# Gates and branches of the token mixers with the tokens' rows as the stationary operand and 512 weight columns moving

## The chip, the cores and the metric

The kernel runs on one core of a Trainium2 chip. The metric is the device time of one execution in microseconds (us). Three runs of the kernel before took 2425.22, 2427.73 and 2429.92 us; the median, 2427.73 us, is what the change is compared with.

## The reference

One decoder layer on 256 tokens of width 2048, all in float32. The part that the change touches is the merge of four token mixers ("branches", each 256 x 512) with sigmoid gates, and the projection behind it:

```python
h = adaLN(RMSNorm(x), c)                               # 256 x 2048
proj = h @ w_in                                        # nine slices of 512 columns feed four mixers
branches = (s5(...), hgrn2(...), stick_breaking(...), pool(...))     # each 256 x 512
terms = [sigmoid(h @ w_gate[n]) * (yb @ w_branch[n])   # w_gate[n] 2048 x 2048, w_branch[n] 512 x 2048
         for n, yb in enumerate(branches)]
merged = terms[0] + terms[1] + terms[2] + terms[3]     # 256 x 2048
x = x + gate_mix(c) * (merged @ w_out)                 # w_out 2048 x 2048
h = adaLN(RMSNorm(x), c); x = x + gate_ffn(c) * PEER(h)   # product-key experts; then a final RMSNorm
```

## The kernel before

**Layout and arithmetic.** Activations lie transposed: channels on the 128 partitions, tokens along the free axis, so `h` is 16 tiles of 128 channels x 256 tokens. A float32 product is made of three passes in the fp32r format. A weight tile of 128 x 1024 (512 KB) is loaded as `raw`, ScalarE copies it rounded to `hi` (line 186), VectorE subtracts to get `lo` (line 187); the helper is `split`. The activations are kept as `h_hi` and `h_lo` (the tile `hh`), the mixers' results as `yb[n]` (high and low, in slabs named `pj`). `gemm` then issues hi x high (line 192), hi x low (line 193) and lo x high (line 195). `raw` has 6 buffers, `hi` 4, `lo` 3; the weights stream through these, so ScalarE and VectorE can run ahead of TensorE by that many tiles and no further.

**Gate stage.** `gate_tile(n, m)` makes 128 gate channels for all 256 tokens: the weights are the stationary operand (128 x 128), 256 token columns move; 16 channel blocks times three passes are 48 matmuls into one PSUM tile (`gate_ps`, pool `psg`, two buffers), and ScalarE's sigmoid (line 826) evicts it. There are 4 x 16 = 64 gate tiles. `branch_tile(n, mq)` makes four such tiles `br_ps` of 12 matmuls each; VectorE multiplies each with the gate straight out of PSUM (lines 843 and 845) and adds into `merged` (line 846). For the last mixer (`n` = 0, the S5 one, worked last) the branch tiles lie in the pool `psv`, and `merged` is split into a high and a low part (`mg`, lines 850 and 851), which the product with `w_out` uses as its moving operand.

**Order.** The mixers are worked in the order 3, 2, 1, 0. A list goes over the 64 gate tiles; after each tile a fixed portion of the mixers' own work (`mixers`, `MIX_RATE`) and of a weight stream on VectorE (`ada`, line 243) is issued, and from the twelfth tile on, after every fourth, a branch of an earlier mixer tile group. Within an engine the framework's scheduler settles the order of what is ready; each engine then works its list strictly in order.

**After it.** `w_out` (16 output tiles `out_ps`, in `psg`), the second norm, the query projection, then the expert stages (`u_ps` and `v_ps`): those already have activations as the stationary operand and 512 weight columns moving, in the same fp32r format.

Of the kernel before, what the change touches and what calls it, by code (L numbers as in the profile page):

```python
# [19 lines left out]
D = 2048  # L20
T = 256
# [105 lines left out]
def emit(tc, ap, out):  # L127
# [8 lines left out]
    with ExitStack() as top:  # L136
# [139 lines left out]
        with ExitStack() as p1:  # L276
# [9 lines left out]
            def slab(dt=F32, shape=(128, 4, T)):  # L286
                return pj.tile(list(shape), dt, tag="pj", name="pj")
# [529 lines left out]
            merged = c1.tile([128, KT, T], F32, name="merged")  # L817
# [3 lines left out]
            def gate_tile(n, m):  # L821
                ps = psg.tile([128, T], F32, tag="g", name="gate_ps")
                gemm_tile(ps, ap["w_gate"][n, m],
                          lambda k: h_hi[:, k], lambda k: h_lo[:, k])
                sg = tp.tile([128, T], F32, tag="sig", name="sig", bufs=12)
                act(sg, ps, AF.Sigmoid)
                sig[n, m] = sg

            def branch_tile(n, mq):
                yh, yl = yb[n]  # L830
                for i in range(4):
                    m = 4 * mq + i
                    if i % 2 == 0:
                        hi, lo = split(ap["w_branch"][n, mq, i // 2])
                        hi = hi.rearrange("p (k m) -> p k m", k=4)
                        lo = lo.rearrange("p (k m) -> p k m", k=4)
                    msl = slice(i % 2 * 128, i % 2 * 128 + 128)
                    ps = (psg if n else psv).tile([128, T], F32, tag="v" if n == 0 else "g", name="br_ps")
                    gemm(ps, lambda k: hi[:, k, msl], lambda k: lo[:, k, msl],
                         lambda k: yh[:, k], lambda k: yl[:, k], range(4))  # L840
                    sg = sig.pop((n, m))
                    if n == 3:
                        tt(merged[:, m], sg, ps, op=ALU.mult)
                    else:
                        tt(sg, sg, ps, op=ALU.mult)
                        tt(merged[:, m], merged[:, m], sg, op=ALU.add)
                    if n == 0:
                        if i == 0:
                            mg[mq], mg[4 + mq] = slab(F32R), slab(F32R)
                        act(mg[mq][:, i], merged[:, m], AF.Copy)  # L850
                        tt(mg[4 + mq][:, i], merged[:, m], mg[mq][:, i].bitcast(F32),
                           op=ALU.subtract)
# [10 lines left out]
            order = [(n, m) for n in (3, 2, 1, 0) for m in range(KT)]  # L863
            for i in range(64 + 9):
                if i < 64:
                    gate_tile(*order[i])
                    mixers(MIX_RATE)
                    ada(ADA_RATE(i))
                if i >= 11 and (i - 11) % 4 == 0:
                    n, m = order[i - 11]  # L870
                    while n in left:
                        mixers.one()
                    branch_tile(n, m // 4)
# [16 lines left out]

            for m in range(KT):
                if m % 4 == 0:
# [3 lines left out]
                ps = psg.tile([128, T], F32, tag="g", name="out_ps")  # L896
                gemm_tile(ps, ap["w_out"][m],
                          lambda k: mg[k // 4][:, k % 4], lambda k: mg[4 + k // 4][:, k % 4])
# [455 lines left out]
def layout(i):  # L1354
# [11 lines left out]
    a["w_gate"] = f(i["w_gate"][0].reshape(4, KT, 128, KT, 128).transpose(0, 3, 2, 1, 4).reshape(4, KT, 128, 2048))  # L1366
    for n, k in (("w_out", "w_out"), ("w_query", "peer_w_query")):
        a[n] = f(i[k][0].reshape(KT, 128, KT, 128).transpose(2, 1, 0, 3).reshape(KT, 128, 2048))
    a["w_branch"] = f(i["w_branch"][0].reshape(4, 4, 128, 4, 2, 256).transpose(0, 3, 4, 2, 1, 5)
# [60 lines left out]
```

## Time and profile before

| what | value |
|---|---|
| median of three runs | 2427.73 us |
| the profiled execution | 2424.11 us, span 2422.3 us |
| TensorE busy | 2344.1 us, 97% of the span |
| VectorE busy | 2044.9 us, 84% |
| ScalarE busy | 1194.6 us, 49% |
| gate stage (first `gate_ps` to last `br_ps`) | 295.7 to 845.9 us |
| `w_out` | 844.5 to 946.7 us |
| DMA over the span | 678.43 MB, 280 GB/s |

[...] What a matmul costs in a stream is the distance from its start to the start of the next. The busy share of TensorE therefore says only that it is hardly ever left without work, and the time of an edit on it has to be read from start to start in a timeline. The other engines' busy times are plain.

### The profile page before, as it was taken

How to read it: one execution, taken by the hardware profiler on the slowest of the kernel's cores; microseconds unless marked ns; L12 is line 12 of the kernel's file. 1: busy time of each engine (PE TensorE's matmuls, PEld its weight loads, DVE VectorE, ACT ScalarE, POOL GpSimd, SP SyncE). 2: the span in 40 equal slices, each digit the busy share in tenths (PEclk: the TensorE clock that was granted, in tenths of full speed). 3: DMA queues.
4: the chain of work that ended last, by engine and by line, in shares of the span. 5: the costliest groups of instructions: out<-in, count | busy, mean ns of one | idle time of the engine just before them, and what ended most of it. 6: DMA issues, size and time to landing. Idle time of an engine off the chain costs nothing.

```text
span 2422.3 us, 39431 instructions
## 1 busy us (share of the span) xinstructions
PE 2344.1 (97%) x15282; PEld 2039.8 (84%) x15282; DVE 2044.9 (84%) x2999; ACT 1194.6 (49%) x1511; POOL 196.6 (8%) x132
## 2 busy tenths in 40 slices
PE   6999999999999999999899999999999999999997
PEld 4789999999999998988688888888888877878875
DVE  6666988779999887899977788888877899988986
ACT  4333466644444445555455544455555444455545
POOL 0000000000000000000122200011122101111110
PEclk9999999999999999999999999999999999999999
DMA  8977888866676686567799976789999767899973
GB/s 310 340 258 265 309 267 268 269 228 229 231 252 236 225 298 226 192 183 255 276 374 358 351 261 244 257 334 350 368 351 350 269 231 247 305 343 357 345 266 125
DMA packets 171724, 678.43 MB, mean 280 GB/s; under 512 B 18880, under 2 KB 23760, under 8 KB 154704
## 3 DMA queue, kind: packets, MB, share of 16 engines
q1 hardware_dynamic: 153104, 541.68, 64.1%
q0 software_dynamic: 18432, 134.23, 14.5%
q8 instruction: 120, 1.97, 0.3%
q14 instruction: 68, 0.56, 0.1%
HBM read 671.07 MB, written 4.20 MB: 279 GB/s over the span
## 4 chain that ended last, share of the span: by engine, by line
PE 82%; DVE 8%; DMA 5%; ACT 2%; issue 2%; SPq 0%; DVEq 0%; ACTq 0%
PE u_ps L1170 14%; PE u_ps L1175 9%; PE v_ps L1223 5%; PE v_ps L1224 5%; PE v_ps L1225 5%; PE v_ps L1228 5%; PE v_ps L1231 5%; DMA raw<-in_dram 4%; PE gate_ps L192 4%; PE gate_ps L193 3%; PE gate_ps L195 3%; PE w_ps L1141 3%; DVE lo L187 3%; PE psw_in L192 3%; PE psw_in L195 2%; PE psw_in L193 2%
## 5 line engine op out<-in xcount | busy, mean ns | idle before, releaser
L186 ACT ACTIVATE hi<-raw 128x1024 fp32r<-128x1024 f32 x808 | 854.9, 1060 | 1017.8 <-DMA raw<-in_dram 240.6
L187 DVE TENSOR_TENSOR lo<-raw,hi 128x1024 fp32r<-128x1024 f32 x808 | 978.3, 1219 | 199.0 <-ACT hi L186 170.2
L1097 POOL DMA_INDIRECT gat<-in_dram,sidx x128 | 196.4, 1534 | 2120.9 <-ACT ring L1196 1125.8
L1170 PE MATMUL u_ps<-hi,hd 128*128 128x512 f32 x1024 | 290.7, 402 | 0.6 <-ACT late L1184 0.6
L192 PE MATMUL gate_ps<-hh,hi 128*128 128x256 f32 x1024 | 256.0, 287 | 0.0
L193 PE MATMUL gate_ps<-hh,hi 128*128 128x256 f32 x1024 | 252.9, 284 | 0.0
L1170 PEld LDWEIGHTS u_ps<-hi,hd 128*128 128x128 f32 x1024 | 193.3, 195 | 39.9 <-ACT late L1184 6.7
L1223 PE MATMUL v_ps<-hi,ph 128*128 128x512 f32 x512 | 207.9, 408 | 6.1 <-DVE late L1240 3.4
L1225 PE MATMUL v_ps<-hi,ph 128*128 128x512 f32 x512 | 202.6, 396 | 0.0
L1224 PE MATMUL v_ps<-hi,ph 128*128 128x512 f32 x512 | 202.1, 395 | 0.0
L192 PEld LDWEIGHTS gate_ps<-hh,hi 128*128 128x128 f32 x1024 | 197.7, 193 | 3.1 <-issue 2.2
L243 DVE SCALAR_TENSOR_TENSOR pj<-raw,csil,pj 128x1024 f32<-128x1024 f32 x135 | 172.3, 1277 | 31.9 <-DMA raw<-in_dram 31.3
L193 PEld LDWEIGHTS gate_ps<-hh,hi 128*128 128x128 f32 x1024 | 197.8, 193 | 0.1
L1170 PE MATMUL u_ps<-lo,hd 128*128 128x512 f32 x512 | 163.6, 400 | 7.8 <-DVE lo L187 7.8
L1228 PE MATMUL v_ps<-lo,ph 128*128 128x512 f32 x512 | 162.9, 396 | 0.6 <-DVE lo L187 0.6
L1231 PE MATMUL v_ps<-lo,ph 128*128 128x512 f32 x512 | 162.8, 396 | 0.0
L1175 PE MATMUL u_ps<-hi,hd 128*128 128x512 f32 x512 | 161.5, 394 | 0.0
L1175 PE MATMUL u_ps<-lo,hd 128*128 128x512 f32 x512 | 159.5, 392 | 0.0
L1120 DVE SCALAR_TENSOR_TENSOR rows<-gat,dots,rows 128x2048 f32<-128x2048 f32 x63 | 147.7, 2345 | 0.0
L1110 DVE SCALAR_TENSOR_TENSOR gat<-gat,hrow 128x2048 f32<-128x2048 f32 x64 | 146.1, 2283 | 0.0
L195 PE MATMUL gate_ps<-hh,lo 128*128 128x256 f32 x1024 | 145.1, 284 | 0.0
L195 PEld LDWEIGHTS gate_ps<-hh,lo 128*128 128x128 f32 x1024 | 133.0, 193 | 0.3
(390 smaller groups left out, 4053.7 us busy)
## 6 DMA issues: line engine op xcount, KB each, us to landing
raw<-in_dram SPq DMA_DIRECT2D x1002, 512.0 KB
pj<-in_dram SPq DMA_DIRECT2D x10, 512.0 KB
x2d<-pj SPq DMA_DIRECT2D x4, 512.0 KB
ring<-in_dram SPq DMA_DIRECT2D x2, 1024.0 KB
gat<-in_dram,sidx POOLq DMA_INDIRECT x128, 8.3
xr<-x2d SPq DMA_DIRECT2D x8, 256.0 KB
ring<-g2d SPq DMA_DIRECT2D x1, 1024.0 KB
out_dram<-ring SPq DMA_DIRECT2D x4, 256.0 KB
```

Source lines behind the costliest of these rows:

```text
L186: act(hi, raw, AF.Copy)
L187: last["lo"] = tt(lo, raw, hi.bitcast(F32), op=ALU.subtract)
L192: mm(ps, hi(n), aH(k), start=start and n == 0, stop=False)
L193: mm(ps, hi(n), aL(k), start=False, stop=False)
L195: mm(ps, lo(n), aH(k), start=False, stop=stop and n == len(ks) - 1)
L1170: mm(ps0, hd[:, 2 * kk + i, 64:ND, r], w[:, i * 512:i * 512 + 512], start=kk == 0 and i == 0 and r == 0 and w is hi, stop=kk == 7 and i == ...
L1175: mm(ps1, hd[:, 2 * kk + i, 0:64].rearrange("p t r -> p (t r)"), w[:, i * 512:i * 512 + 512], start=kk == 0 and i == 0 and w is hi, stop=k ...
L1223: mm(vps[dq], phl[:, i, 0:128, 1], hi[:, dsl], start=first, stop=False)
L1224: mm(vps[dq], phl[:, i, 0:128, 0], hi[:, dsl], start=False, stop=False)
L1225: mm(vps[2 + dq], phl[:, i, 128:192].rearrange("p t r -> p (t r)"), hi[:, dsl], start=first, stop=False)
L1228: mm(vps[2 + dq], phl[:, i, 128:192].rearrange("p t r -> p (t r)"), lo[:, dsl], start=False, stop=last)
L1231: mm(vps[dq], phl[:, i, 0:128, 0], lo[:, dsl], start=False, stop=last)
```

## The change

The gates and the branches are turned round. A unit is 512 gate channels of one mixer, and it holds both halves of the tokens at once: two PSUM tiles of 128 tokens x 512 channels, which are all of `psg`. The stationary operand is 128 channels x 128 tokens of `h_hi` or `h_lo`, the moving one 512 columns of `hi` or `lo`. A unit takes 8 weight tiles and 96 matmuls; there are 16 units in place of 64 gate tiles. In the last of its 8 weight tiles the first token half is finished before the second. A branch unit takes 2 weight tiles and 24 matmuls, and its two PSUM tiles come from `psg` too (from `psv` for the last mixer). Sigmoids, products and sums are 128 x 512. `merged` then has tokens on the partitions, so 64 TensorE transposes of 128 x 128 turn it back (`turned`), and the split into `mg` reads their PSUM tiles. The transposes of the last quarter stand behind the first halves of two `w_out` tiles. The mixers' portions are issued after every second weight tile, which is the same pace as before. The weights lie in DRAM in the new order; bytes and number of loads are the same.

```diff
-            merged = c1.tile([128, KT, T], F32, name="merged")
+            merged = c1.tile([128, 2, D], F32, name="merged")
             mg = [None] * 8
             sig = {}
 
-            def gate_tile(n, m):
-                ps = psg.tile([128, T], F32, tag="g", name="gate_ps")
-                gemm_tile(ps, ap["w_gate"][n, m],
-                          lambda k: h_hi[:, k], lambda k: h_lo[:, k])
-                sg = tp.tile([128, T], F32, tag="sig", name="sig", bufs=12)
-                act(sg, ps, AF.Sigmoid)
-                sig[n, m] = sg
-
-            def branch_tile(n, mq):
+            def rows_gemm(ps, t, hi, lo, aH, aL, ks, start, stop, parts=(0, 1)):
+
+                tsl = slice(t * 128, t * 128 + 128)
+                for i, k in enumerate(ks):
+                    w = hi[:, i * 512:i * 512 + 512]
+                    if 0 in parts:
+                        mm(ps, aH(k)[:, tsl], w, start=start and i == 0, stop=False)
+                        mm(ps, aL(k)[:, tsl], w, start=False, stop=False)
+                if 1 in parts:
+                    for i, k in enumerate(ks):
+                        mm(ps, aH(k)[:, tsl], lo[:, i * 512:i * 512 + 512], start=False,
+                           stop=stop and i == 1)
+
+            def gate_unit(n, m4, side):
+                ps = [psg.tile([128, 512], F32, tag="g", name="gate_ps") for _ in range(2)]
+                aH, aL = lambda k: h_hi[:, k], lambda k: h_lo[:, k]
+                for u in range(8):
+                    hi, lo = split(ap["w_gate"][n, m4, u])
+                    ks = range(2 * u, 2 * u + 2)
+                    for p in ((0, 1),) if u == 7 else ((0,), (1,)):
+                        for t in range(2):
+                            rows_gemm(ps[t], t, hi, lo, aH, aL, ks, u == 0, u == 7, p)
+                    if u % 2:
+                        side()
+                for t in range(2):
+                    sig[n, m4, t] = tp.tile([128, 512], F32, tag="sig", name="sig", bufs=6)
+                    act(sig[n, m4, t], ps[t], AF.Sigmoid)
+
+            def turned(m4):
+
+                mg[m4], mg[4 + m4] = slab(F32R), slab(F32R)
+                for j in range(2):
+                    ps = psv.tile([128, 2, T], F32, tag="v", name="mg_ps")
+                    for i in range(2):
+                        d0 = m4 * 512 + j * 256 + i * 128
+                        for t in range(2):
+                            nc.tensor.transpose(ps[:, i, t * 128:t * 128 + 128],
+                                                merged[:, t, d0:d0 + 128], ident)
+                    sl = slice(2 * j, 2 * j + 2)
+                    act(mg[m4][:, sl], ps, AF.Copy)
+                    tt(mg[4 + m4][:, sl], ps, mg[m4][:, sl].bitcast(F32), op=ALU.subtract)
+
+            def branch_unit(n, m4):
                 yh, yl = yb[n]
-                for i in range(4):
-                    m = 4 * mq + i
-                    if i % 2 == 0:
-                        hi, lo = split(ap["w_branch"][n, mq, i // 2])
-                        hi = hi.rearrange("p (k m) -> p k m", k=4)
-                        lo = lo.rearrange("p (k m) -> p k m", k=4)
-                    msl = slice(i % 2 * 128, i % 2 * 128 + 128)
-                    ps = (psg if n else psv).tile([128, T], F32, tag="v" if n == 0 else "g", name="br_ps")
-                    gemm(ps, lambda k: hi[:, k, msl], lambda k: lo[:, k, msl],
-                         lambda k: yh[:, k], lambda k: yl[:, k], range(4))
-                    sg = sig.pop((n, m))
+                parts = [split(ap["w_branch"][n, m4, u]) for u in range(2)]
+                pool, tag = (psg, "g") if n else (psv, "v")
+                ps = [pool.tile([128, 512], F32, tag=tag, name="br_ps") for _ in range(2)]
+                for t in range(2):
+                    for u in range(2):
+                        rows_gemm(ps[t], t, *parts[u], lambda k: yh[:, k], lambda k: yl[:, k],
+                                  range(2 * u, 2 * u + 2), u == 0, u == 1)
+                    sg = sig.pop((n, m4, t))
+                    dst = merged[:, t, m4 * 512:m4 * 512 + 512]
                     if n == 3:
-                        tt(merged[:, m], sg, ps, op=ALU.mult)
+                        tt(dst, sg, ps[t], op=ALU.mult)
                     else:
-                        tt(sg, sg, ps, op=ALU.mult)
-                        tt(merged[:, m], merged[:, m], sg, op=ALU.add)
-                    if n == 0:
-                        if i == 0:
-                            mg[mq], mg[4 + mq] = slab(F32R), slab(F32R)
-                        act(mg[mq][:, i], merged[:, m], AF.Copy)
-                        tt(mg[4 + mq][:, i], merged[:, m], mg[mq][:, i].bitcast(F32),
-                           op=ALU.subtract)
+                        tt(sg, sg, ps[t], op=ALU.mult)
+                        tt(dst, dst, sg, op=ALU.add)
...
-            order = [(n, m) for n in (3, 2, 1, 0) for m in range(KT)]
-            for i in range(64 + 9):
-                if i < 64:
-                    gate_tile(*order[i])
-                    mixers(MIX_RATE)
-                    ada(ADA_RATE(i))
-                if i >= 11 and (i - 11) % 4 == 0:
-                    n, m = order[i - 11]
+            order = [(n, m4) for n in (3, 2, 1, 0) for m4 in range(4)]
+            beat = iter(range(64))
+
+            def step():
+                mixers(MIX_RATE)
+                ada(ADA_RATE(next(beat)))
+
+            for j in range(16 + 2):
+                if j < 16:
+                    gate_unit(*order[j], step)
+                if j >= 2:
+                    n, m4 = order[j - 2]
+                    if n == 0 and m4 > 0:
+                        turned(m4 - 1)
                     while n in left:
                         mixers.one()
-                    branch_tile(n, m // 4)
+                    branch_unit(n, m4)
...
+            ops = {}
             for m in range(KT):
                 if m % 4 == 0:
                     xq = slab()
                     load(out=xq, in_=ap["xT"][:, m:m + 4, :])
                     x2.append(xq)
-                ps = psg.tile([128, T], F32, tag="g", name="out_ps")
-                gemm_tile(ps, ap["w_out"][m],
-                          lambda k: mg[k // 4][:, k % 4], lambda k: mg[4 + k // 4][:, k % 4])
+                for i, halves in (((0, (0,)), (1, (0,)), (0, (1,))) if m == 0 else
+                                  ((1, (1,)),) if m == 1 else ((m, (0, 1)),)):
+                    if halves[0] == 0:
+                        ops[i] = psg.tile([128, T], F32, tag="g", name="out_ps")
+                    elif m == 0:
+                        turned(3)
+                    gemm_tile(ops[i], ap["w_out"][i],
+                              lambda k: mg[k // 4][:, k % 4], lambda k: mg[4 + k // 4][:, k % 4],
+                              halves)
+                ps = ops.pop(m)
...
-    a["w_gate"] = f(i["w_gate"][0].reshape(4, KT, 128, KT, 128).transpose(0, 3, 2, 1, 4).reshape(4, KT, 128, 2048))
+    a["w_gate"] = f(i["w_gate"][0].reshape(4, 8, 2, 128, 4, 512).transpose(0, 4, 1, 3, 2, 5)
+                    .reshape(4, 4, 8, 128, 1024))
-    a["w_branch"] = f(i["w_branch"][0].reshape(4, 4, 128, 4, 2, 256).transpose(0, 3, 4, 2, 1, 5)
+    a["w_branch"] = f(i["w_branch"][0].reshape(4, 2, 2, 128, 4, 512).transpose(0, 4, 1, 3, 2, 5)
```

On TensorE, here a branch of the second mixer and the gate tile or unit behind it. Before, each PSUM tile has its own name in the list, and the gate's one tile follows:

```order
L195 MATMUL br_ps_5816<-pj_3298,lo_5798 128x256 x4
L192 MATMUL gate_ps_5831<-hh_89,hi_5834 128x256
L193 MATMUL gate_ps_5831<-hh_89,hi_5834 128x256
...
L195 MATMUL gate_ps_5831<-hh_89,lo_5835 128x256 x8
```

Now (the first tile of each pair is the first token half, the second the second):

```order
L831 MATMUL br_ps_4945<-lo_4942,pj_3219 128x512 x2
...
L831 MATMUL br_ps_4946<-lo_4942,pj_3219 128x512 x2
L827 MATMUL gate_ps_4975<-hi_4979,hh_89 128x512
L828 MATMUL gate_ps_4975<-hi_4979,hh_89 128x512
...
L831 MATMUL gate_ps_4975<-lo_4980,hh_89 128x512 x2
L827 MATMUL gate_ps_4976<-hi_4979,hh_89 128x512
```

Where two PSUM tiles took turns, both now go to the gate unit at once: six matmuls into `gate_ps_4975` stand between the branch's last matmul and the first into `gate_ps_4976`, the buffer that VectorE has to have emptied of `br_ps_4946`.

On VectorE, the emptying of the same branch and what stands between. Before:

```order
L845 TENSOR_TENSOR sig_4840<-sig_4840,br_ps_5801 128x256
L643 SCALAR_TENSOR_TENSOR pj_5751<-hg_o_5577,col_105,pj_5751 128x256
L846 TENSOR_TENSOR merged_3059<-merged_3059,sig_4840 128x256
L845 TENSOR_TENSOR sig_4926<-sig_4926,br_ps_5816 128x256
L645 TENSOR_TENSOR pj_5751<-pj_5751,pj_151 128x256
L846 TENSOR_TENSOR merged_3059<-merged_3059,sig_4926 128x256
L187 TENSOR_TENSOR lo_6000<-raw_5997,hi_5999 128x1024
```

Now:

```order
L877 TENSOR_TENSOR sig_4404<-sig_4404,br_ps_4945 128x512
L647 TENSOR_TENSOR pj_4863<-pj_4921,pj_4862 128x512
L878 TENSOR_TENSOR merged_3059<-merged_3059,sig_4404 128x512
L187 TENSOR_TENSOR lo_4998<-raw_4995,hi_4997 128x1024
L877 TENSOR_TENSOR sig_4406<-sig_4406,br_ps_4946 128x512
L187 TENSOR_TENSOR lo_5118<-raw_5115,hi_5117 128x1024
L878 TENSOR_TENSOR merged_3059<-merged_3059,sig_4406 128x512
```

Two evictions of 512 columns stand where four of 256 stood, with a weight tile's `lo` between them.

On ScalarE, a gate's sigmoid and the weight tiles of later work that are rounded ahead of it. Before, behind the gate tile's own last weight tile `hi_5864`:

```order
L186 ACTIVATE hi_5999<-raw_5997 128x1024
L186 ACTIVATE hi_6029<-raw_6027 128x1024
L646 ACTIVATE pj_5665<-pj_5751 128x512
L186 ACTIVATE hi_6121<-raw_6119 128x1024
L186 ACTIVATE hi_6151<-raw_6149 128x1024
L826 ACTIVATE sig_5892<-gate_ps_5831 128x256
```

Now, behind the unit's own last weight tile `hi_5280`:

```order
L186 ACTIVATE hi_5342<-raw_5340 128x1024
L186 ACTIVATE hi_5348<-raw_5346 128x1024
L186 ACTIVATE hi_5386<-raw_5384 128x1024
L847 ACTIVATE sig_5336<-gate_ps_4975 128x512
L757 ACTIVATE pj_5297<-pj_5180 128x4x32
```

The sigmoid has moved from behind four later weight tiles to behind three. Between the last matmul of the first token half and the branch that follows, in the list of TensorE, stand five matmuls at least and mostly six to ten.

## Rows read from the trace of the kernel before

**Rows 1.** The page: TensorE's busy line, and the chain that ended last by engine.

```profile
PE 2344.1 (97%) x15282; PEld 2039.8 (84%) x15282; DVE 2044.9 (84%) x2999; ACT 1194.6 (49%) x1511; POOL 196.6 (8%) x132
PE 82%; DVE 8%; DMA 5%; ACT 2%; issue 2%; SPq 0%; DVEq 0%; ACTq 0%
```

**Rows 2.** Busy time in two stretches of the gate stage; columns in the first line.

```profile
core 0: us, PE busy (x) PEld busy (x) DVE busy (x) ACT busy (x) POOL busy (x), PEclk, DMA share, GB/s
296.00:540.00 244.00, 235.79 (x2305) 232.06 (x2304) 198.51 (x262) 152.19 (x185) 0.00 (x0) 1.00 0.78 257
540.00:790.00 250.00, 248.55 (x1969) 234.19 (x1968) 238.55 (x402) 111.49 (x169) 0.00 (x0) 0.99 0.70 238
```

**Rows 3.** Timeline of TensorE, half a gate tile: start, duration, line, tiles, count.

```profile
708.88 0.28 PE L192 MATMUL gate_ps<-hh,hi 128*128 128x256 f32 x1
...
710.80 1.12 PE L195 MATMUL gate_ps<-hh,lo 128*128 128x256 f32 x8
711.76 0.28 PE L192 MATMUL gate_ps<-hh,hi 128*128 128x256 f32 x1
```

**Rows 4.** Timeline of TensorE in the first expert stage, one weight tile.

```profile
1303.81 1.09 PE L1170 MATMUL u_ps<-hi,hd 128*128 128x512 f32 x4
...
1306.12 1.09 PE L1170 MATMUL u_ps<-hi,hd 128*128 128x512 f32 x4
```

**Rows 5.** Timeline of TensorE in the second expert stage, one weight tile.

```profile
2187.38 0.40 PE L1223 MATMUL v_ps<-hi,ph 128*128 128x512 f32 x1
...
2189.72 0.40 PE L1223 MATMUL v_ps<-hi,ph 128*128 128x512 f32 x1
```

**Rows 6.** Timeline of TensorE, four float32 transposes between the expert stages.

```profile
1586.30 0.60 PE L1191 MATMUL t_ps<-cst,late 128*128 128x128 f32 x4
1586.65 0.49 PE L1223 MATMUL v_ps<-hi,ph 128*128 128x512 f32 x1
1586.98 0.39 PE L1224 MATMUL v_ps<-hi,ph 128*128 128x512 f32 x1
```

**Rows 7.** Groups of instructions from 296 to 846: busy us, mean ns, idle before.

```profile
L192 PE MATMUL br_ps<-pj,hi 128*128 128x256 f32 x256 | 66.1, 292 | 7.6 <-DVE merged L843 4.9 <-ACT sig L826 2.3 <-ACT s5sg L811 0.4
L826 ACT ACTIVATE sig<-gate_ps 128x256 f32<-128x256 f32 x64 | 24.1, 377 | 29.0 <-PE gate_ps L195 28.7
L826 ACT ACT_TABLE_LOAD x18 | 23.1, 1283 | 0.3
L845 DVE TENSOR_TENSOR sig<-sig,br_ps 128x256 f32<-128x256 f32 x46 | 18.7, 413 | 3.8 <-PE br_ps L195 3.7
L846 DVE TENSOR_TENSOR merged<-merged,sig 128x256 f32<-128x256 f32 x46 | 18.5, 415 | 0.0
L781 DVE TENSOR_TENSOR s5a<-s5bu,pj 128x512 f32<-128x512 f32 x16 | 10.9, 683 | 2.0 <-PE s5bu L778 1.9
L851 DVE TENSOR_TENSOR pj<-merged,pj 128x256 fp32r<-128x256 f32 x13 | 5.3, 416 | 0.5 <-ACT pj L850 0.5
L639 ACT ACTIVATE pj<-hg_s 128x512 f32<-128x512 f32 x2 | 1.2, 595 | 1.3 <-PE hg_s L637 1.3
```

**Rows 8.** Groups of the whole program: the same transposes' mean duration.

```profile
L1191 PE MATMUL t_ps<-cst,late 128*128 128x128 f32 x128 | 19.3, 272 | 0.0
```

**Rows 9.** Timeline: a branch tile's last matmuls, and VectorE's eviction of it.

```profile
653.71 0.64 PE L195 MATMUL br_ps<-pj,lo 128*128 128x256 f32 x4
...
655.82 0.72 DVE L845 TENSOR_TENSOR sig<-sig,br_ps 128x256 f32<-128x256 f32 x2
```

**Rows 10.** Timeline: a gate tile's last matmuls, its sigmoid, the branch behind it.

```profile
684.42 1.12 PE L195 MATMUL gate_ps<-hh,lo 128*128 128x256 f32 x8
...
688.39 0.38 ACT L826 ACTIVATE sig<-gate_ps 128x256 f32<-128x256 f32 x1
...
688.83 0.38 PE L192 MATMUL br_ps<-pj,hi 128*128 128x256 f32 x1 [0.80 <-ACT sig L826]
```

## The prediction

> **What bounds the kernel now.** I began with the page: TensorE is busy 97% of the span, and the chain that ended last runs over it for 82% [rows 1]. A busy share that high leaves two questions, what a matmul costs from start to start and which other engine is close behind. The busy times of two stretches of the gate stage answer the second [rows 2]: from 296 to 540 us VectorE is busy 198.5 of 244 us and TensorE 235.8, so TensorE alone sets the pace; from 540 to 790 us, where the S5 mixer's work runs beside the gates, VectorE is busy 238.6 of 250 us, 95%, and TensorE 248.6. [...] The timeline gives the first answer: half a gate tile is 24 matmuls of 256 columns, and the next half starts 2.88 us after it [rows 3], 0.1200 us each. The idle time before the branches' matmuls is 7.6 us in all, put down to evictions of the PSUM tiles [rows 7]; the gates show none.
>
> **The matmuls.** Removed: 64 gate tiles of 48 and 64 branch tiles of 12, together 3840 of 256 columns; 3840 x 0.1200 = 460.8 us. Added: 16 units of 96 and 16 of 24, together 1920 of 512 columns. The kernel already has that form, activations stationary and 512 weight columns moving, each block of columns used by two matmuls in a row. In the first expert stage ten of them take 2.31 us, 0.2310 each [rows 4]; in the second 2.34 us, 0.2340 each [rows 5]. The product is 443.5 or 449.3 us. Nothing in the two stages says which the gates resemble more, so I take the middle, 0.2325 us: 446.4 us. That is **-14.4 us**, with ends -17.3 and -11.5. Pairs of 256 cost 0.240 and one of 512 costs 0.2325; half as many instructions buys only 3%. All of it lies on the engine that sets the end.
>
> **The transposes.** Added: 64 on TensorE, float32, 128 x 128. The nearest row is one of the same form: four transposes and one 512-column matmul behind them take from 1586.30 to 1586.98 us, 0.68 us [rows 6]. Less 0.234 for the matmul that is 0.446 us for four, 0.1115 each, and 64 make **+7.1 us**. The lower end is the four alone, 0.35 us, so 5.6 us in all. The upper end is no overlap at all: a mean duration of 272 ns [rows 8], 17.4 us. I take 7.1, since the starts show that they overlap.
>
> **The evictions.** On VectorE 64 products and 48 sums of 256 columns at 413 and 415 ns become 32 and 24 of 512 columns at 683 ns, the duration of a product out of PSUM of that size [rows 7]: 46.4 us become 38.2. The low parts of `merged` are 16 at 416 ns and become 8 at 683, 6.7 to 5.5. VectorE loses 9.4 us of work. On ScalarE 64 sigmoids at 377 ns become 32 at 595 (a copy out of PSUM of that size) [rows 7], 24.1 to 19.0, beside 18 table loads of 1.283 us which can only become fewer. I count all this as nothing, because TensorE's work covers it; if VectorE should be the one that binds from 540 us on, its own relief there is 0.6 us a unit (four products and four sums of 256 columns against two and two of 512), which is the first rival below.
>
> **The waits at the hand-over of PSUM.** A unit now holds both buffers of `psg`. Behind a branch the next unit's second half needs the buffer that VectorE empties last. Six matmuls stand between, 1.40 us. The result is there about 0.17 us after the last matmul's turn (a duration of 0.40 against a distance of 0.234 [rows 5]), and the product takes 0.683: VectorE may come 0.55 us late before TensorE stops. If it stops, the whole list behind it waits, and with it ScalarE and VectorE, once the four `hi` and three `lo` are full. There are 12 such places. The trace shows VectorE prompt at some and late at others: a branch tile that ended at 654.35 us was taken up at 655.82, 1.47 us late [rows 9]. The price at one place is between 0 and 0.92 us; I take 0.3, nearer to the prompt end, because VectorE has as a rule already waited for the first half of the same branch. Together 3.6 us, between 0 and 11.0.
>
> Before a branch, and between the first units, it is ScalarE that must have emptied the first half. With six matmuls between, 0.17 for the result and 0.595 for the sigmoid, it may come 0.63 us late. There are 14 such places. The trace has a gate tile that ended at 685.54 us and whose sigmoid began at 688.39, 2.85 us late, with 0.80 us of wait for the branch [rows 10]; behind the new order that would be 2.22 us. The sigmoid has moved forward by one weight tile in ScalarE's list, so I take 0.2 us a place, 2.8 us; the ends are 0 and, with half the places as late as that one, 15.5 us. In return the 7.6 us of old waits go. **-1.2 us** in all, between -7.6 and +18.9.
>
> **The rest.** Loads keep their number and size. The last quarter's transposes stand behind 31 matmuls of `w_out`, 3.7 us by 0.1200 each, in which the last product and sum, 0.17 + 0.683 + 0.683 = 1.5 us, fit with a weight tile's work between: nothing, and up to 2 us if VectorE comes late.
>
> **Sum.** -14.4 + 7.1 - 1.2 = -8.5 us. The profiled execution took 2424.11 us (its span 2422.3, with 1.8 around it) and would take 2415.6. It lies 3.6 us below the median of the runs, 2427.73; carried over to the median, the forecast is **2419 us**, 0.35% faster. A measurement of this kernel can tell about 0.2%, 4.9 us, from no change: faster is below 2422.9, slower above 2432.6.
>
> **Rivals.** *VectorE binds beside the S5 mixer.* At 95% busy for 250 of the stage's 550 us [rows 2], it could hold that stretch to its old length. Then the share 250/550 of 14.4 us, 6.5 us, is lost, and the sum is -2.0: 2426 us, no change. For it speaks the 95%; against it that TensorE is at 99% in the same stretch and that VectorE is relieved too.
>
> *The hand-over waits decide.* One mechanism: two halves that share two buffers stop TensorE at each unit's edge until VectorE or ScalarE has come round. With VectorE as late as in [rows 9] at all 12 places and ScalarE as late as in [rows 10] at seven of 14, the waits are 11.0 + 15.5 = 26.5 us and the sum is -14.4 + 7.1 + 26.5 - 7.6 = +11.6: 2439 us, slower. It makes the kernel slower than can be called no change from 19.8 us of waits on, 0.76 us at each of 26 places. For it speaks that lateness of 1 us and more is there in the trace; against it that the order now puts six matmuls and more into each gap.
>
> *The transposes do not overlap.* At 272 ns each [rows 8] they cost 17.4 us in place of 7.1, and the sum is +1.8: 2430 us. Against it speaks the distance of starts in [rows 6].
>
> [...]
>
> **Chances.** The forecast has 0.47, with its own range from 2410 to 2424; VectorE binding 0.27; the hand-over waits 0.18; the transposes 0.08. Of the forecast 0.43 lies below 2422.9 and 0.04 above; of VectorE's case 0.02 is faster, 0.23 the same, 0.02 slower; the waits are slower; of the transposes 0.05 is the same, 0.03 slower. So faster 0.45, same 0.32, slower 0.23. The best ends of all terms give -17.3 + 5.6 - 7.6 = -19.3, 2408 us; the worst -11.5 + 17.4 + 18.9 + 2 = +26.8, 2455 us. The range from 2407 to 2441 leaves out the worst part of the two slow cases.
>
> **What would show it.** Starts of `gate_ps` matmuls 0.231 to 0.234 us apart, against 0.120 for half the columns; more than 0.236 makes the first step wrong, and at 0.240 it is worth nothing. Groups of eight `mg_ps` transposes near 0.9 us. Idle time in front of `gate_ps` and `br_ps` matmuls near 6 us and put down to VectorE's products or ScalarE's sigmoids; above 20 us the second rival has won. If the starts are as forecast, the waits small and the stage from the first gate to the last branch still about 550 us long with VectorE at 97% or more from 540 us on, VectorE binds.

## The result, and the profile after

Six runs of the changed kernel have a median of 2411.23 us (2405.55 to 2415.05); six of the kernel before, on the same chip, 2427.85 us. The ratio is 0.9933, 95% interval 0.992 to 0.9945: 16.6 us faster. A second set on another chip gave 2412.31 us, ratio 0.9925 (0.9907 to 0.9944). The profiled run took 2414.72 us (span 2412.9), the profile of the second set has a span of 2409.1.

TensorE's line of the page, in place of the one in [rows 1], and the two stretches of [rows 2] again:

```profile
PE 2332.8 (97%) x13394; PEld 1942.4 (81%) x13394; DVE 2039.8 (85%) x2935; ACT 1173.5 (49%) x1458; POOL 199.4 (8%) x132
```

```profile
296.00:540.00 244.00, 232.57 (x1461) 190.24 (x1460) 198.52 (x251) 133.05 (x156) 0.00 (x0) 0.97 0.76 258
540.00:790.00 250.00, 245.85 (x1143) 189.24 (x1142) 242.39 (x383) 114.36 (x158) 0.00 (x0) 0.99 0.71 242
```

TensorE has 1888 records fewer and is still busy 97%. Yet it works less in both stretches than before (232.57 against 235.79, 245.85 against 248.55): it waits more. In the first one the granted clock has gone from 1.00 to 0.97. The groups from 295 to 838 us, which answer to [rows 7]:

```profile
L827 PE MATMUL gate_ps<-hi,hh 128*128 128x512 f32 x512 | 206.1, 403 | 10.3 <-DVE merged L875 6.4 <-ACT sig L847 3.9
L827 PE MATMUL br_ps<-hi,pj 128*128 128x512 f32 x128 | 52.7, 414 | 6.0 <-ACT sig L847 4.9 <-ACT pj L813 1.1
L847 ACT ACTIVATE sig<-gate_ps 128x512 f32<-128x512 f32 x32 | 18.4, 593 | 3.8 <-PE gate_ps L831 3.7
L877 DVE TENSOR_TENSOR sig<-sig,br_ps 128x512 f32<-128x512 f32 x23 | 15.6, 680 | 3.3 <-PE br_ps L831 3.0
L847 ACT ACT_TABLE_LOAD x11 | 14.1, 1283 | 0.2
```

Sigmoids and products cost what the rows of before had said (593 and 680 ns). The idle time before gates and branches has gone from 7.6 us to 16.3, and the gates, which had none, have most of it. Over the whole gate stage TensorE waited 11.7 us before, 16.7 now, and 15.9 in the second set.

The timeline of TensorE around one of the three long waits (start, duration, line, tiles, count, idle time before and what ended it):

```profile
612.36 0.39 PE L827 MATMUL gate_ps<-hi,hh 128*128 128x512 f32 x1
612.59 0.39 PE L828 MATMUL gate_ps<-hi,hh 128*128 128x512 f32 x1
612.81 0.39 PE L827 MATMUL gate_ps<-hi,hh 128*128 128x512 f32 x1
613.04 0.39 PE L828 MATMUL gate_ps<-hi,hh 128*128 128x512 f32 x1
613.27 0.61 PE L831 MATMUL gate_ps<-lo,hh 128*128 128x512 f32 x2
617.68 0.79 PE L827 MATMUL br_ps<-hi,pj 128*128 128x512 f32 x1 [3.80 <-ACT sig L847]
618.27 0.63 PE L828 MATMUL br_ps<-hi,pj 128*128 128x512 f32 x1
618.70 0.63 PE L827 MATMUL br_ps<-hi,pj 128*128 128x512 f32 x1
619.12 0.63 PE L828 MATMUL br_ps<-hi,pj 128*128 128x512 f32 x1
```

From 612.36 to 613.27 us four matmuls start 0.2275 us apart, though each lasts 0.39; the median over all 1920 is 0.227, less than either price of [rows 4, 5]. Then the branch waits 3.80 us for a sigmoid. Behind the wait the starts are 0.43 us apart, nearly twice as far, and the stretches of the profile say why (here the first wait, at 324 us; the column behind the busy times is the granted clock):

```profile
323.20:330.03 6.83, 6.00 (x14) 4.74 (x15) 5.15 (x7) 5.71 (x7) 0.00 (x0) 0.50 0.85 315
330.03:333.00 2.97, 2.97 (x14) 2.44 (x14) 0.41 (x2) 0.85 (x1) 0.00 (x0) 1.00 0.48 177
```

For 6.83 us the clock was granted at 0.50, then at 1.00. Such a stretch stands behind each of the three waits. Its first 0.8 to 0.9 us still lie in the wait, and of the other 6 us about half is lost, 3.0 us (by the starts, 0.43 us apart in place of 0.227, it is 2.8). The gate stage has three of them now, 20.5 us in all (10.2 in the second set). The gate stage of before has one, 6.8 us from 636.6 us on, with no wait in the 8 us ahead of it: TensorE was busy all of that time, from 635.09 us on with 16 matmuls of a single column, 13 of which began ahead of the stretch. So a wait is not the only thing in front of such a stretch.

The three waits have three causes. At 617.68 ScalarE comes late, behind eight scaled copies of the S5 mixer (line 765) and a table load:

```profile
612.86 2.86 ACT L765 ACTIVATE s5e<-pj,s5pw 128x128 f32<-128x128 f32 x8
615.74 1.28 ACT L847 ACT_TABLE_LOAD   x1
617.03 1.08 ACT L847 ACTIVATE sig<-gate_ps 128x512 f32<-128x512 f32 x2
```

At 324.03 (3.71 us) it is ScalarE too, with two table loads around the stick-breaking mixer's own function ahead of the sigmoid. At 487.93 it is VectorE, whose product (line 875) stands in its list behind a weight stream (line 243) that waits 3.33 us for its load:

```profile
484.86 1.28 DVE L243 SCALAR_TENSOR_TENSOR pj<-raw,csil,pj 128x1024 f32<-128x1024 f32 x1 [3.33 <-DMA raw<-in_dram]
486.06 1.22 DVE L187 TENSOR_TENSOR lo<-raw,hi 128x1024 fp32r<-128x1024 f32 x1
487.20 0.68 DVE L875 TENSOR_TENSOR merged<-sig,br_ps 128x512 f32<-128x512 f32 x1
```

The transposes, eight of a quarter and the branch behind them:

```profile
816.70 1.03 PE L857 MATMUL mg_ps<-cst,merged 128*128 128x128 f32 x8
817.49 0.48 PE L827 MATMUL br_ps<-hi,pj 128*128 128x512 f32 x1
817.81 0.40 PE L828 MATMUL br_ps<-hi,pj 128*128 128x512 f32 x1
```

From 816.70 to 817.81 us are 1.11 us; less 0.227 for the branch's matmul, 0.110 us for each transpose. There are four such groups, 32 transposes. The 64 of the section on the change and of the prediction was a miscount: four quarters, two PSUM tiles, two channel blocks and two token halves are 32.

**The sum.** At the median distance, 1920 x 0.227 = 435.8 us stand against 460.8: -25.0. But in either kernel some hundred of these matmuls, most of them next to a matmul of other work or to a wait, take 0.06 us or more longer than that to the next start. Added up from start to start, without idle time and without what the slow clock cost (estimated as half of each stretch, less its part in a wait), the gates and branches fall from 470.2 us to 449.4 (449.7 in the second set): -20.8 and -20.5. The whole gate stage, from the timelines, in us:

| first `gate_ps` to last `br_ps` | before | changed | second set |
|---|---|---|---|
| length | 550.2 | 543.0 | 538.8 |
| gates and branches, start to start | 470.2 | 449.4 | 449.7 |
| idle time of TensorE | 11.7 | 16.7 | 15.9 |
| lost to the slow clock | 3.4 | 8.9 | 5.0 |
| transposes (24 of the 32) | 0 | 2.2 | 2.2 |
| first matmuls of `w_out` | 0.3 | 2.3 | 2.3 |
| the mixers' own matmuls | 64.7 | 63.5 | 63.6 |

Of the span, shorter by 9.4 us (13.2 in the second set), 7.2 (11.4) lie in this stage and 1.7 (1.8) behind it. The medians lie further apart, by 16.6 us: the profiled run of before was 3.7 us faster than its median, that of the changed kernel 3.5 us slower than its own. What a middle run of before had more of is not known, since there is one profile of it.

### The profile page after: what moved, and what is told of

Its sections match the earlier page's. It is cut to its first block, busy times and chain, and to the rows that moved or that the text cites. A ratio compares the mean times of both kernels' runs of the same rounds, so it can differ in the third digit from the quotient of the medians.

```text
span 2412.9 us, 35538 instructions
## 1 busy us (share of the span) xinstructions
PE 2332.8 (97%) x13394; PEld 1942.4 (81%) x13394; DVE 2039.8 (85%) x2935; ACT 1173.5 (49%) x1458; POOL 199.4 (8%) x132
## 5 line engine op out<-in xcount | busy, mean ns | idle before, releaser
L827 PE MATMUL gate_ps<-hi,hh 128*128 128x512 f32 x512 | 206.1, 403 | 10.3 <-DVE merged L875 6.4
L828 PE MATMUL gate_ps<-hi,hh 128*128 128x512 f32 x512 | 202.7, 396 | 0.0
L831 PE MATMUL gate_ps<-lo,hh 128*128 128x512 f32 x512 | 144.9, 394 | 0.4 <-DVE lo L187 0.3
L827 PEld LDWEIGHTS gate_ps<-hi,hh 128*128 128x128 f32 x512 | 97.8, 191 | 36.7 <-DVE merged L875 9.0
L1263 PEld LDWEIGHTS v_ps<-hi,ph 128*128 128x128 f32 x512 | 101.3, 198 | 30.7 <-issue 4.5
L192 PE MATMUL psw_in<-hh,hi 128*128 128x256 f32 x448 | 117.6, 292 | 6.7 <-ACT hi L186 6.4
```

Of the source, the lines that this page charges most:

```text
L827: mm(ps, aH(k)[:, tsl], w, start=start and i == 0, stop=False)
L828: mm(ps, aL(k)[:, tsl], w, start=False, stop=False)
L1263: mm(vps[dq], phl[:, i, 0:128, 1], hi[:, dsl], start=first, stop=False)
```

## The experiments

Four theories. **H**: TensorE sets the pace of the gate stage, and what the change lost it lost at the hand-over of the two buffers. **V**: VectorE binds beside the S5 mixer. **T**: a transpose costs its duration. For the price of 0.227 us: **S**, the stationary operand of the gates lies with unit step, that of the expert stages every second element; **B**, other traffic in those stages slows them; and later **A**, the places of the operands in memory. The changed kernel again, beside the first four:

> The changed kernel itself, timed beside the variants on the same chip. Theory H (hand-over waits and the slow-clock stretches behind them hold part of the gain back, and differ from run to run): runs between 2404 and 2416 us, the longer ones with the lower mean granted clock. Rival: a single time within 0.1%, so that the profiled run's longer time needs another cause.

Its runs took 2407.33 to 2413.82 us, the shortest at a mean granted clock of 0.990 and the three longest at 0.987 and 0.988, as H expected.

**Three buffers in place of two** (and three for the mixers in place of four), up to the expert stages:

```diff
-psg = top.enter_context(tc.tile_pool(name="psg", bufs=2, space=PSUM))
-psv = top.enter_context(tc.tile_pool(name="psv", bufs=4, space=PSUM))
...
+psg = p1.enter_context(tc.tile_pool(name="psg1", bufs=3, space=PSUM))
+psv = p1.enter_context(tc.tile_pool(name="psv1", bufs=3, space=PSUM))
```

> Three PSUM buffers for gates and branches in place of two, three in place of four for the mixers; everything else as in the changed kernel. Theory H: the long waits in front of gate_ps and br_ps (3.7, 3.1 and 3.8 us in the changed kernel's trace) shrink to under 1 us each, the slow-clock stretches behind them (6.8 us each) go, and the time falls by 8 to 15 us. Rival V (VectorE's work sets the pace from 540 us on): the time stays within 4 us, as the waits come back elsewhere.

Measured 2404.49 us (2402.22 to 2406.25), 0.9894 (0.9877 to 0.9912): 7.8 us less than the changed kernel, and the runs of the two do not overlap. Its groups and its longest wait:

```profile
L827 PE MATMUL gate_ps<-hi,hh 128*128 128x512 f32 x512 | 202.2, 395 | 2.0 <-ACT hi L184 1.0 <-ACT sig L847 1.0
L827 PE MATMUL br_ps<-hi,pj 128*128 128x512 f32 x128 | 52.6, 412 | 4.8 <-ACT sig L847 3.0 <-DVE pj L861 0.8 <-DVE sig L877 0.7
```

```profile
PE hg_s L637 <- DVE pj L630: 3.1, 1, 3.1
```

The gates' idle time falls from 10.3 us to 2.0, and two of the three long waits go under 1 us; the branch at 605 us still waits 2.95 us for its sigmoid. So the hand-over did cost, as H says. But part of it comes up again at once in the mixers (3.1 us at line 637): the gate stage's whole idle time falls only from 15.9 to 13.6, and of the 6.2 us between the two profiles the stage itself gives 2.4, what lies between it and the expert stages 2.1, and the part ahead of the gates 3.8 (from the expert stages on it took 2.1 more). In the profiles without this edit the gates began anywhere from 291.3 to 296.6 us, so those 3.8 us can't be put down to it. That the 7.8 us all come from the hand-over is not shown.

**Four buffers** (and two for the mixers):

```diff
+psg = p1.enter_context(tc.tile_pool(name="psg1", bufs=4, space=PSUM))
+psv = p1.enter_context(tc.tile_pool(name="psv1", bufs=2, space=PSUM))
```

> Four PSUM buffers for gates and branches, two for the mixers (the two sums of squares of the second norm are allocated at the end of the stage in place of before it). Theory H: waits in front of gate_ps and br_ps near zero, 10 to 18 us less than the changed kernel, unless the mixers wait for their two buffers. Rival V: within 4 us of the changed kernel.

Measured 2413.53 us (2412.06 to 2416.67), 0.9935: nothing gained, where H gave 10 to 18 us. Waits of TensorE in the gate stage (total, times, longest):

```profile
PE gate_ps L831 <- DVE lo L185: 4.4, 4, 1.8
PE hg_s L637 <- DVE pj L630: 3.2, 1, 3.2
PE sb_o L505 <- DVE pj L499: 1.6, 2, 1.4
```

No gate waits for an eviction any more; TensorE waits for the high and low parts of the weights and in the mixers instead, 21.1 us in all against 15.9. Where the hand-over no longer held TensorE, the next wait did, and other engines ended that one.

**The transposes, each issued twice:**

```diff
+for _ in range(2):
     nc.tensor.transpose(ps[:, i, t * 128:t * 128 + 128], merged[:, t, d0:d0 + 128], ident)
```

> Each of the 32 transposes of the merged rows is issued twice into the same place; nothing else changes. Theory H: the 32 stand on the path of the end and cost their distance of starts, 0.109 us each, so 32 more cost 3.5 us: about 2416 us on a chip where the changed kernel takes 2412. Rival T (transposes do not overlap, price 0.272 us, their duration): 8.7 us, about 2421 us. Rival C (they are hidden beside waits for the last quarter's evictions): under 1 us. 64 mg_ps matmuls in the trace, in groups of eight.

Measured 2415.62 us (2413.94 to 2422.66), 3.3 us more than the changed kernel in its second set; by the ratios, 0.9947 (0.9925 to 0.9969) against 0.9925, it is 5.3, so the time alone doesn't settle it. The timeline does:

```profile
812.94 1.91 PE L858 MATMUL mg_ps<-cst,merged 128*128 128x128 f32 x16
814.61 0.48 PE L827 MATMUL br_ps<-hi,pj 128*128 128x512 f32 x1
814.93 0.40 PE L828 MATMUL br_ps<-hi,pj 128*128 128x512 f32 x1
```

Sixteen take 1.99 - 0.227 = 1.76 us, again 0.110 each, while one lasts 0.272. T is refuted: the duration is not the price, which in a group of eight or sixteen was 0.4 of it.

**More work on TensorE alone**, in the first or in the last half of the gate stage. A fourth product, low by low, is added:

```diff
+if n in (3, 2) and u % 2 == 0 and 1 in p:     # the other run: n in (1, 0)
+    for i, k in enumerate(ks):
+        mm(ps[t], aL(k)[:, t * 128:t * 128 + 128], lo[:, i * 512:i * 512 + 512], start=False, stop=False)
```

> The fourth product, low part by low part, is added for every second weight tile of the gates of the first two mixers worked (3 and 2): 128 more matmuls of 512 columns, from 295 to about 556 us, and no work on any other engine. Theory H (TensorE sets the pace in the whole gate stage, 0.227 us a matmul): +29 us, about 2441 us. Rival V concerns the other half of the stage and expects the same here, +29. If the waits at the hand-over take part, it is less by as much as they shrink (the largest three, 3.7 + 3.1 + 3.8 us and a slow stretch behind each): 20 to 29.

> The same 128 extra matmuls, but in the gates of the last two mixers worked (1 and 0), from about 556 to 817 us, where VectorE is busy 95% of the time. Theory H: TensorE sets the pace here too, +29 us less the share of the waits that vanish, the same as for the first two mixers within 4 us: about 2438 to 2441 us. Rival V (VectorE binds beside the S5 mixer): TensorE has some 6 to 15 us of slack there which the extra matmuls fill, +14 to +23 us: 2426 to 2435 us, clearly less than with the first two mixers.

Measured 2433.26 us (2426.53 to 2438.76), 1.0012 (0.9999 to 1.0025), and 2432.12 us (2428.41 to 2436.95), 1.0007 (0.9992 to 1.0021): +20.9 and +19.8 us for 29.1 of matmuls. The two halves do not differ by more than the intervals, so VectorE's 96 to 97% in the second half binds it no more than its 81 to 83% in the first. This comparison speaks against V, although 2432 us alone lies in the range that V gave for the second half, and below that of H. In both about a third of the added work is free by the medians, which H at its plainest did not say. The gates of the first of the two runs:

```profile
L827 PE MATMUL gate_ps<-hi,hh 128*128 128x512 f32 x512 | 203.5, 398 | 8.5 <-DVE merged L879 5.4 <-ACT sig L851 3.1
L827 PE MATMUL br_ps<-hi,pj 128*128 128x512 f32 x128 | 51.6, 404 | 0.5 <-ACT sig L851 0.5
```

The waits before gates and branches are 9.9 us, of 15.9, and the stage has one slow stretch of 3.4 us in place of three. Against the second set's profile the stage is 21.9 us longer for 29.4 us more of matmuls from start to start; its whole idle time is 5.3 us less, and the slow clock costs 3.3 less. Whether the added work caused this is not shown: two profiles of the changed kernel differ by 3.9 us in what the slow clock costs. In the second run the stage is 24.6 us longer, and its matmuls add 25.9 us in place of 29.1, since fewer of the gates' matmuls take longer than the median; waits (13.5 us) and slow stretches (13.7 us) together give nothing back. Why fewer of them do stays open.

**The stationary operand of the first expert stage with unit step:**

```diff
-hd = c2.tile([128, KT, ND, 2], F32R, name="hd")       # high and low parts interleaved
+hd = c2.tile([128, KT, 2 * ND], F32R, name="hd")      # low of the last 128, high of all, low of the middle 64
...
-mm(ps0, hd[:, 2 * kk + i, 64:ND, r], w[:, i * 512:i * 512 + 512],
+mm(ps0, hd[:, 2 * kk + i, 256 - 256 * r:384 - 256 * r], w[:, i * 512:i * 512 + 512],
```

> First expert stage: the stationary operands of u_ps lie with unit step in SBUF (before: high and low parts interleaved, step two for the first of the two PSUM tiles); the turning matrix of its second tile follows. Theory S (the step of the stationary operand is why a 512-column matmul costs 233 ns there and 227 ns in the gates): L1210's distance of starts falls from 233 to 227 to 230 ns, 1536 x 4 to 6 ns, 6 to 9 us less than the changed kernel. Rival B (the traffic of that stage, 350 GB/s against 240, is why): 233 ns stay, time unchanged.

Measured 2403.08 us (2400.53 to 2406.5), 0.989 (0.9872 to 0.9908), 9.2 us less than the changed kernel. One weight tile of that stage (ten matmuls) in the changed kernel, and in this one:

```profile
1303.87 1.09 PE L1210 MATMUL u_ps<-hi,hd 128*128 128x512 f32 x4
1306.18 1.09 PE L1210 MATMUL u_ps<-hi,hd 128*128 128x512 f32 x4
```

```profile
1304.08 1.07 PE L1212 MATMUL u_ps<-hi,hd 128*128 128x512 f32 x4
1306.34 1.07 PE L1212 MATMUL u_ps<-hi,hd 128*128 128x512 f32 x4
```

2.31 us become 2.26: the six matmuls that read every second element go from 0.233 to 0.227, by the medians of the whole stage. S holds for them. The other four, which had unit step before too, go from 0.228 to 0.230 down to 0.227 as well; why is open. From the stage's first matmul to its last 842.0 us become 835.3 in the two profiles, so 6.7 of the 9.2 us are accounted for. A step of two cost 6 ns of 233 there.

**The same in both expert stages** (the second stage's low part is then written by two instructions of VectorE, 0.42 and 0.29 us, in place of one of 0.55):

```diff
-phl = pp.tile([128, 2, ND, 2], F32R, tag="ph", name="ph")
+phl = pp.tile([128, 2, 2 * ND], F32R, tag="ph", name="ph")
...
```

> In both expert stages the stationary operand lies with unit step in SBUF (before: every second element, since high and low parts are interleaved); the low part of the second stage's operand is then written by two VectorE instructions in place of one. Theory S (a step of two in the stationary operand costs the matmul 6 us per thousand): u_ps starts 0.227 us apart as in the earlier run and v_ps too, from 0.231-0.234; with some 2500 v_ps matmuls up to 14 us beyond the 9 us that the first stage alone gave, less what VectorE's extra instructions cost: 2390 to 2398 us. Rival B (the difference of 0.227 and 0.233 comes from other traffic in the stage): v_ps stays at 0.231 to 0.234, about 2403 us.

Measured 2407.74 us (2404.64 to 2410.16), 0.9909 (0.9891 to 0.9927) on another chip: nothing beyond the first stage's gain, rather less of it. `v_ps` stays at 0.233 to 0.234, so S does not explain the second stage. One thing in the layout still set it apart from the gates: its operand begins on a multiple of 64 bytes, theirs 32 past one, as all weight tiles do; that 64 bytes are the measure was the author's assumption. Hence theory A, and 32 bytes of padding:

```diff
+padp = p2.enter_context(tc.tile_pool(name="padp", bufs=1))
+nc.vector.memset(padp.tile([128, 8], F32, name="padp_t"), 0.0)
 pp = p2.enter_context(tc.tile_pool(name="pp", bufs=2))
```

> As the earlier run with unit steps in both expert stages, and 32 bytes of padding ahead of the second stage's operand tile, so that it begins 32 bytes past a multiple of 64 in each partition, as the stationary tiles of the gates and of the first stage do; before it began on the multiple itself, half a step off the weight tiles, which all begin 32 past. Theory A (where the stationary operand begins, against a multiple of 64 or against the moving operand, costs the other 6 us per thousand): v_ps starts go from 0.233 to 0.227 us, 2560 x 0.0063 = -16 us against that run's 2407.7: about 2392 us. Rival B (other traffic of the stage): v_ps stays at 0.233, 2407 us.

Measured 2410.68 us (2406.85 to 2412.12), 0.9914 (0.9898 to 0.9929), and `v_ps` is where it was: six matmuls in 1.40 us, 0.233 each.

```profile
1900.31 0.39 PE L1267 MATMUL v_ps<-hi,ph 128*128 128x512 f32 x1
...
1901.71 0.63 PE L1272 MATMUL v_ps<-lo,ph 128*128 128x512 f32 x2
```

A fails for the second expert stage; why that stage keeps to 0.233 stays open. For the gates themselves, the same padding once around their stationary tile alone, and once ahead of it and all that follows:

```diff
+padh = top.enter_context(tc.tile_pool(name="padh", bufs=1))
+nc.vector.memset(padh.tile([128, 8], F32, name="padh_t"), 0.0)
 hpool = top.enter_context(tc.tile_pool(name="hpool", bufs=1))
+padr = top.enter_context(tc.tile_pool(name="padr", bufs=1))           # in the first of the two alone
+nc.vector.memset(padr.tile([128, 8], F32, name="padr_t"), 0.0)
```

> The changed kernel, with the gates' stationary tile alone moved by 32 bytes (it begins on a multiple of 64, the weight tiles 32 past one); all else lies as it was, against multiples of 64. Theory A: gate_ps starts 0.233 us apart in place of 0.227, br_ps still 0.227; 1536 x 0.0063 = +9.7 us, about 2422 us. Rival B: gate_ps stays at 0.227, 2412 us.

> The changed kernel with the gates' stationary tile and everything behind it in memory moved by 32 bytes, the weight tiles too. Theory A1 (what counts is where stationary and moving tile lie against each other): gate_ps and br_ps stay at 0.227 us, v_ps stays at 0.231 to 0.234; 2412 us. Theory A2 (what counts is the stationary tile against multiples of 64): gate_ps and br_ps go to 0.233 (+12 us), the part of v_ps with unit step to 0.227 (1024 x 0.0063 = -6.5 us), the like part of u_ps from 0.229 to 0.233 (+4 us): about 2422 us. Rival B: all as before, 2412 us, and the run with the gates' tile alone moved is at 0.227 too.

Ten matmuls of a gate with its tile moved alone, then eight with all moved:

```profile
700.20 0.40 PE L831 MATMUL gate_ps<-hi,hh 128*128 128x512 f32 x1
...
702.54 0.39 PE L831 MATMUL gate_ps<-hi,hh 128*128 128x512 f32 x1
```

```profile
699.86 0.39 PE L829 MATMUL gate_ps<-hi,hh 128*128 128x512 f32 x1
...
701.67 0.39 PE L829 MATMUL gate_ps<-hi,hh 128*128 128x512 f32 x1
```

Moved alone, 2.34 us for ten, 0.234 each (the branches, not moved, stay at 0.227); moved together, 1.81 for eight, 0.226. So in the gates A1 holds: with the stationary tile moved 32 bytes against the weight tile a matmul cost 7 ns more, with both moved no more, and at both places tried it is their distance that counts. The times, though, are 2412.76 us (2409.01 to 2414.2), 0.9918 (0.9899 to 0.9937), and 2410.75 us (2409.25 to 2412.46), 0.9913 (0.9894 to 0.9932), four runs each: no difference clear of the intervals. From start to start the gates and branches take 456.8 us in the first and 448.5 in the second, so of 8.3 us more of matmuls 2.0 show. Idle time and what the slow clock cost are 13.8 + 5.0 us in the first, 17.2 + 8.8 in the second, 7.2 us less; that the slower matmuls caused this is not shown.

**All together**, three buffers, unit steps and the padding:

> The same with three gate buffers in place of two, which alone took 7.8 us off. Theories A and H together: 2384 us. If B holds, 2400 us.

Measured 2404.3 us (2401.97 to 2406.81), 0.9885 (0.9869 to 0.9901), 20 us above what A and H gave together: the lowest ratio of all, but not below three buffers alone (0.9894) or the first stage's unit step alone (0.989) by more than the intervals. Against the run with unit steps and padding but two buffers, on the same chip (2410.68 us), three buffers gave 6.4 us, near the 7.8 of the first time. What did not come again is the 9.2 us of the first expert stage: with unit steps in both stages the ratios are 0.9909 and 0.9914, against 0.9925 for the changed kernel and 0.9913 for the changed kernel with all tiles moved, which ran on the same chip as the 0.9914. The stage itself is shorter each time (835.8 to 837.1 us from its first matmul to its last, against 841.1 and 842.0), so 4 to 6 us hold there; where the program takes part of that back is open.

## Why the prediction was right or wrong

The forecast, 2419 us and faster, had the sign right, and its range held the time; the gain is twice the forecast. By the profiles of the two sets the matmuls gave -20.8 and -20.5 us in place of -14.4, the transposes +3.5 in place of +7.1, waits and slow clock +10.5 and +5.8 in place of -1.2; the rest, -2.6 and -2.0, is in the mixers' matmuls and outside of the stage. Two terms were too dear and one too cheap, so that the total came as near as it did is in part luck.

- **The matmuls**: one of 512 costs less than two of 256, as said, but the price is 0.227 us, not 0.2325. The term is -25.0 at the medians and -20.8 and -20.5 from start to start, both beyond the end of -17.3; what some matmuls take longer next to other work or a wait (9.4 us in all before, 13.6 now) had no place in it. The step that failed is "Nothing in the two stages says which the gates resemble more, so I take the middle". Something did: the kernel's lines show which operands are read with a step of two. [rows 4] mixes six such matmuls with four of unit step, and the gates have unit step. In the profile of before the six start 0.233 us apart and the four 0.229 to 0.230, which would have made the term -19 to -21. That the gates came down to 0.227 no row of before shows; their tiles also lie alike, and the moved tile showed that this matters to them (0.234).
- **The transposes**: the price of [rows 6], 0.1115, was right (0.110), the number was wrong by two: +3.5, not +7.1.
- **The waits**: forecast -1.2, the old 7.6 us going and 6.4 coming. In the two profiles they are idle time, +5.0 and +4.2, and slow clock, +5.5 and +1.6, which the forecast did not have at all. The step "I take 0.3" a place, an even lateness, failed in kind. The 16.7 us of idle time less the three long waits are 6.1, close to the 3.6 + 2.8 of the forecast; but three places cost 3.0 to 3.8 us each, where ScalarE or VectorE stands in order behind something long. The lateness of [rows 10], 2.85 us, was the better guide for these.
- **The evictions** at nothing: their durations came out as read (593 and 680 ns); that they are hidden but for the places above is argued from the waits, not tested.
- **VectorE binds beside the S5 mixer** was wrong, as far as the comparison of the two halves goes: added matmuls cost there what they cost in the other. **The transposes do not overlap** was wrong. **The hand-over waits decide** named the right mechanism, but it took 10.6 us at three places, not 26.5 at 19.

What the forecast had no place for: at 97% busy, TensorE's own work is not the whole price. Of the 8.3 us that the moved tile added 2.0 reached the end, of 29.1 us added 20.9 and 19.8. In two of these three profiles shorter waits and fewer slow stretches stand against it, but such stretches differ as much between two profiles of one kernel.

## What to carry to other kernels

Take the price of a matmul from one whose operands lie alike in memory (step, and start against the moving tile), since here 0.227 us in place of 0.2325 made 10.6 us. And add up the starts of the stage, not only its medians: 1920 of them came to 13.6 us more than the median says. Before sharing two PSUM buffers between both halves of a tile, look in the evicting engines' lists for what stands ahead of each eviction (table loads, a stream that waits for its load): a few long waits, not a mean over all places, set the cost here (three, 10.6 of 16.7 us). And expect the next engine to take back part of what a nearly full one gains, as with three buffers, where the gates' idle time fell from 10.3 us to 2.0 and the whole stage's only from 16.7 to 13.6.

## What was not expected of the hardware

- A step of two in the stationary operand made a 512-column matmul 0.233 us in place of 0.227 in the first expert stage, and a start moved 32 bytes against the weight tile's made it 0.234 in place of 0.227 in the gates; in the second expert stage neither mattered (0.233 to 0.234 throughout).
- Behind the waits of 3.71, 3.05 and 3.80 us in the gate stage TensorE's granted clock was 0.50 for 6.8 us each. Not behind every wait: behind those of 2.26 us, ended at 329.92, and 2.15 us, ended at 487.32, in the kernel before it stayed at 1.00. And not only there: in the kernel before it was 0.50 for 6.8 us from 636.6 us on, with no wait in the 8 us ahead. What decides it is open.
